# A third seven-product k pair in the gate and up projections, and three low parts formed by an accumulating DMA

## The chip, the core and the metric

The kernel runs on one core of a Trainium2 chip. The metric is the device time of one execution in microseconds (us). The core's engines are TensorE (PE in the profile, PEld for its weight loads), VectorE (DVE), ScalarE (ACT), GpSimd (POOL) and SyncE (SP); 16 DMA engines move data. SP issues the loads of the weights. GpSimd issues some small DMAs in software.

## What is computed

A trunk of two decoder layers over 256 positions of width 2048, all in float32:

```python
for layer in range(2):
    h = h + mixer(rms_norm(h, norm_mix[layer]))   # 0: sliding window + mLSTM, 1: forgetting attention
    xn = rms_norm(h, norm_ffn[layer])
    h = h + (silu(xn @ w_gate[layer]) * (xn @ w_up[layer])) @ w_down[layer]
return rms_norm(h, norm_final)
```

`w_gate` and `w_up` are 2048 x 5632, `w_down` is 5632 x 2048. The change concerns the products with `w_gate` and `w_up` alone.

## The kernel before, in words

**Two parts for one float32.** Every large product is made from operands split into a high part, the number rounded to TensorE's float32r format (`hi`), and a low part, what the rounding left (`lo = raw - hi`). A product is three matmuls: x-high with w-high, x-high with w-low, x-low with w-high (`gemm`, L164 to L166; `three`, L345 to L347).

**Chunks.** A weight chunk is two k tiles of 128 rows by 512 columns, 512 KB. `load_raw` (L85) loads it from SP's queue into one of four `raw` buffers (pool `wr`). `split_chunk` (L138) forms `hi` on ScalarE (L141) and `lo` on VectorE (L142), in pools of four buffers each (`wp`). So a load waits until a `raw` buffer has been read for the last time, a split until a `hi` and a `lo` buffer have been used for the last time by TensorE, and a matmul until its parts are there. SP issues its loads in order: one that waits holds back those behind it.

**The gate and up stage.** `ffn` (L416) cuts the 5632 columns into 11 groups of 512, in two parts of 6 and 5 groups, each part followed by its share of the product with `w_down`. `gate_up` (L352) makes one group: gate and up for both row tiles t (128 positions each), over 16 k tiles taken as eight pairs. `ORDER` (L34) says in which order, and of which kind each pair is:

- A *plain* pair (flag 0) loads one chunk of gate and one of up, splits both and runs 2 matrices x 2 k tiles x 2 row tiles x 3 = 24 matmuls.
- A *mixed* pair (flag 1) makes the same eight block products (two k tiles, two matrices, two row tiles) with seven, by a scheme of sums and differences. It loads `rg` and `ru` (L374, L375), splits `rg` as a plain chunk (L376), forms four combined weight blocks `t4` on VectorE (L378 to L381), splits one half of `ru` (L384) and `t4` in two pieces (`ht`, `lt`, L389; `split_plain` is L239 to L241), and runs 7 x 3 = 21 matmuls (L396 to L402). The matching combinations of x (`sh`, `sl`) are made once a layer by `sums_of` (L199), called from `split_scaled` in the output projection. Four of the seven products gather over the mixed pairs in four PSUM banks of their own (`mixed`, called `prod`), and are combined at the end of the group (L405 to L413).

Before, pairs 2 and 3 are mixed, in places three and six of the order; two plain pairs stand between them, two after the second and two ahead of the first. Then follow the activation (L428), the gating (L430), eight transposes (`pf`, L438) and the split of the result (L441). PSUM banks alternate: the plain banks of one group are the mixed banks of the next (`par`).

**Who orders the instructions.** The program is built with a planner that places the instructions of each engine by its own timing model; engines run their queues strictly in order, so the built order, buffer assignment included, is what runs. In this document a chunk is called by pair and matrix: 5u is the up chunk of pair 5, and 6u* one whose low part is made by DMA.

Of the kernel before, what the change touches and what calls it, by code (L numbers as in the profile page):

```python
# [7 lines left out]
F32 = mybir.dt.float32  # L8
F32R = mybir.dt.float32r
AF = mybir.ActivationFunctionType  # L10
ALU = mybir.AluOpType
# [10 lines left out]
NB = 512  # L22
# [8 lines left out]
OFF_QM, OFF_KM, OFF_VM, OFF_OM = 1536, 2048, 2560, 3584  # L31
CAP = 15.0
FILL = 24
ORDER = ((0, 0), (0, 1), (1, 2), (0, 4), (0, 5), (1, 3), (0, 6), (0, 7))  # L34
MIXED = [p for w, p in ORDER if w]
HALVES = (0, 6, 11)

# [2 lines left out]
def trunk(  # L40
# [20 lines left out]
    nc = tc.nc  # L61
# [23 lines left out]
    def load_raw(w, k0, c0, n):  # L85
        raw = wr.tile([P, CK, NB], F32, tag="raw", name="raw")
        nc.sync.dma_start(
            raw[:, :, 0:n], w[k0 * P : (k0 + CK) * P, c0 : c0 + n].rearrange("(k p) n -> p k n", p=P)
        )
        return raw  # L90
# [40 lines left out]
    gain_columns(0)  # L131


    def load_chunk(w, k0, c0, n):
        raw = ahead.pop(0) if ahead else load_raw(w, k0, c0, n)
        return split_chunk(raw, n)

    def split_chunk(raw, n):  # L138
        hi = wp.tile([P, CK, NB], F32R, tag="hi", name="hi")
        lo = wp.tile([P, CK, NB], F32R, tag="lo", name="lo")  # L140
        nc.scalar.copy(hi[:, :, 0:n], raw[:, :, 0:n])  # L141
        nc.vector.tensor_tensor(  # L142
            out=lo[:, :, 0:n], in0=raw[:, :, 0:n], in1=hi[:, :, 0:n].bitcast(F32), op=ALU.subtract
        )
        return hi, lo
# [23 lines left out]
    def x_of(k):  # L169
        return xh[:, k, :], xl[:, k, :]  # L170
# [68 lines left out]
    def split_plain(dst_h, dst_l, src):  # L239
        nc.scalar.copy(dst_h, src)  # L240
        nc.vector.tensor_tensor(out=dst_l, in0=src, in1=dst_h.bitcast(F32), op=ALU.subtract)  # L241
# [102 lines left out]
    def three(o, ah, al, hi, lo, start, stop):  # L344
        nc.tensor.matmul(o, ah, hi, start=start, stop=False)  # L345
        nc.tensor.matmul(o, ah, lo, start=False, stop=False)  # L346
        nc.tensor.matmul(o, al, hi, start=False, stop=stop)  # L347

    def bank(par, name):
        return pm.tile([P, NB], F32, tag="pm", name=name) if par else pa.tile([P, NB], F32, tag="acc", name=name)  # L350

    def gate_up(fp, sh, sl, layer, g, par):  # L352
        c0 = g * NB
        plain = [[bank(par, "acc") for _ in range(NT)] for _ in range(2)]
        mixed = None
        count = [s_[0] for s_ in ORDER]
        for pos, (w, pair) in enumerate(ORDER):
            k0 = 2 * pair
            if not w:
                for m, wt in enumerate((w_gate[layer], w_up[layer])):  # L360
                    hi, lo = load_chunk(wt, k0, c0, NB)
                    for i in range(CK):
                        ah, al = x_of(k0 + i)
                        for t in range(NT):
                            ts = slice(t * P, (t + 1) * P)
                            three(
                                plain[m][t], ah[:, ts], al[:, ts], hi[:, i, :], lo[:, i, :],
                                pos == 0 and i == 0, pos == len(ORDER) - 1 and i == CK - 1,
                            )
                continue  # L370
            first, last = 1 not in count[:pos], 1 not in count[pos + 1 :]
            if first:
                mixed = [bank(1 - par, "prod") for _ in range(4)]
            rg = load_raw(w_gate[layer], k0, c0, NB)  # L374
            ru = load_raw(w_up[layer], k0, c0, NB)  # L375
            hg, lg = split_chunk(rg, NB)  # L376
            t4 = fp.tile([P, 4, NB], F32, tag="t4", name="t4", bufs=1)
            nc.vector.tensor_tensor(out=t4[:, 0, :], in0=ru[:, 0, :], in1=rg[:, 0, :], op=ALU.subtract)  # L378
            nc.vector.tensor_tensor(out=t4[:, 1, :], in0=ru[:, 1, :], in1=ru[:, 0, :], op=ALU.subtract)  # L379
            nc.vector.tensor_tensor(out=t4[:, 2, :], in0=ru[:, 1, :], in1=t4[:, 0, :], op=ALU.subtract)  # L380
            nc.vector.tensor_tensor(out=t4[:, 3, :], in0=rg[:, 1, :], in1=t4[:, 2, :], op=ALU.subtract)  # L381
            hu = wp.tile([P, CK, NB], F32R, tag="hi", name="hi")
            lu = wp.tile([P, CK, NB], F32R, tag="lo", name="lo")
            split_plain(hu[:, 1, :], lu[:, 1, :], ru[:, 1, :])  # L384
            ht, lt = [], []
            for i in range(2):
                hs = fp.tile([P, 2, NB], F32R, tag="ht", name="ht")
                ls = fp.tile([P, 2, NB], F32R, tag="lt", name="lt")
                split_plain(hs, ls, t4[:, 2 * i : 2 * i + 2, :])  # L389
                ht += [hs[:, 0, :], hs[:, 1, :]]  # L390
                lt += [ls[:, 0, :], ls[:, 1, :]]
            j = MIXED.index(pair)
            xa, la = x_of(k0)
            xb, lb = x_of(k0 + 1)
            t0, t1 = slice(0, P), slice(P, 2 * P)
            three(mixed[0], xa[:, t0], la[:, t0], hg[:, 0, :], lg[:, 0, :], first, last)  # L396
            three(plain[0][0], xb[:, t0], lb[:, t0], hg[:, 1, :], lg[:, 1, :], False, False)
            three(plain[1][0], sh[:, j, 3, :], sl[:, j, 3, :], hu[:, 1, :], lu[:, 1, :], False, False)
            three(mixed[1], sh[:, j, 0, :], sl[:, j, 0, :], ht[0], lt[0], first, last)
            three(mixed[2], sh[:, j, 2, :], sl[:, j, 2, :], ht[1], lt[1], first, last)  # L400
            three(mixed[3], sh[:, j, 1, :], sl[:, j, 1, :], ht[2], lt[2], first, last)
            three(plain[0][1], xb[:, t1], lb[:, t1], ht[3], lt[3], False, False)  # L402
        c = fp.tile([P, 4, NB], F32, tag="c", name="c", bufs=1)
        u2 = fp.tile([P, NB], F32, tag="tmp", name="u2")
        nc.scalar.copy(c[:, 0, :], mixed[0])  # L405
        nc.vector.tensor_tensor(out=u2, in0=mixed[3], in1=c[:, 0, :], op=ALU.add)
        nc.vector.tensor_tensor(out=c[:, 1, :], in0=mixed[2], in1=u2, op=ALU.add)
        nc.vector.tensor_tensor(out=c[:, 2, :], in0=mixed[1], in1=u2, op=ALU.add)
        nc.vector.tensor_tensor(out=c[:, 3, :], in0=mixed[1], in1=c[:, 1, :], op=ALU.add)
        for m in range(2):  # L410
            for t in range(NT):
                o = c[:, 2 * m + t, :]
                nc.vector.tensor_tensor(out=o, in0=plain[m][t], in1=o, op=ALU.add)  # L413
        return c

    def ffn(layer, fp, sh, sl, eh, el, key, idx_next=None, key_next=None, finish=None):  # L416
# [4 lines left out]
        for part in range(2):  # L421
            g0, g1 = HALVES[part : part + 2]
            nk = 4 * (g1 - g0)
            for g in range(g0, g1):
                par = (g - g0 + part) % 2
                c = gate_up(fp, sh, sl, layer, g, par)
                for t in range(NT):
                    nc.scalar.activation(c[:, t, :], c[:, t, :], AF.Silu, scale=r[:, t : t + 1])  # L428
                for t in range(NT):
                    nc.vector.scalar_tensor_tensor(  # L430
                        out=c[:, t, :], in0=c[:, 2 + t, :], scalar=r[:, t : t + 1], in1=c[:, t, :], op0=ALU.mult, op1=ALU.mult
                    )
                for half in range(2):
                    pt = bank(par, "pf").rearrange("p (i q) -> p i q", i=2)
                    for i in range(2):
                        cs = (2 * half + i) * P
                        for t in range(NT):
                            nc.tensor.transpose(pt[:, i, t * P : (t + 1) * P], c[:, t, cs : cs + P], ident)  # L438
                    k = 4 * (g - g0) + 2 * half
                    if k < KT:  # L440
                        split_plain(mh[:, k : k + 2, :], ml[:, k : k + 2, :], pt)  # L441
                    else:
                        split_plain(eh[:, k - KT : k - KT + 2, :], el[:, k - KT : k - KT + 2, :], pt)
# [444 lines left out]
```

## Time and profile before

| | us |
|---|---|
| runs of the kernel (median of 3) | 2187.59 (2187.58 to 2188.13) |
| the profiled execution, its own time | 2186.29 |
| its span, first to last instruction | 2184.6 |
| TensorE busy | 2164.8 (99%) |
| VectorE busy | 1442.0 (66%) |
| ScalarE busy | 1078.5 (49%) |
| GpSimd busy | 38.4 (2%) |
| mean busy share of the DMA engines over 40 slices | 0.4 to 0.8, mostly 0.5 to 0.7 |

The granted clock of TensorE was 0.998. "Busy" for TensorE counts a matmul from its start to its modelled end; matmuls overlap, so a full row is no sign of how fast they follow each other. Groups of instructions carry the source line, the operation, the tile written and read, the shape, the count, and the busy time and mean duration of one. A wait names the engine and line that was waited for. For a DMA the profile gives the median time from issue to landing.

### The profile page before, as it was taken

The page shows a single profiled execution, that of the slowest core. Times are in us where ns is not written, and L with a number is a line of the kernel's source. Part 1 is how long each engine was busy: PE and PEld are TensorE (multiplying, and loading weights), DVE is VectorE, ACT ScalarE, POOL GpSimd, SP SyncE. Part 2 cuts the span into 40 slices and gives each one's busy share as a digit, 9 for nine tenths or more (in the row PEclk, how much of TensorE's full clock was granted, in tenths as well). Part 3 has the DMA queues.
Part 4 walks back from the last instruction along what each step waited for, and adds up shares of the span by engine and source line. Part 5 has one row for each costly group of instructions (what it writes and reads, how often), then busy time and mean ns, then how long its engine had stood idle before and what let it go on. Part 6 is the DMA issues. An engine that isn't in the chain of part 4 may idle for free.

```text
span 2184.6 us, 26574 instructions
## 1 busy us (share of the span) xinstructions
PE 2164.8 (99%) x10052; PEld 1796.9 (82%) x10052; DVE 1442.0 (66%) x1732; ACT 1078.5 (49%) x1397; POOL 38.4 (2%) x61
## 2 busy tenths in 40 slices
PE   8999999999999999999999999999999999999998
PEld 6878888888888888888888888888888888888886
DVE  5565566788754677865555555668778645777754
ACT  5565455555543455544545544555455434554543
POOL 2110000000000000000010000000000000000000
PEclk9999999999999999999999999999999999999999
DMA  8544556666666666566675565566666665666664
GB/s 258 150 147 148 171 167 184 203 186 208 187 194 193 201 192 195 190 196 190 176 229 167 164 178 157 177 184 195 208 184 197 198 193 183 208 192 199 194 191 144
DMA packets 213536, 408.33 MB, mean 187 GB/s; under 512 B 12736, under 2 KB 21024, under 8 KB 213152
## 3 DMA queue, kind: packets, MB, share of 16 engines
q1 hardware_dynamic: 212736, 402.90, 60.0%
q0 software_dynamic: 624, 3.72, 0.5%
q8 instruction: 78, 1.28, 0.2%
q14 instruction: 50, 0.41, 0.1%
q10 hardware_dynamic: 48, 0.02, 0.0%
HBM read 404.48 MB, written 2.11 MB: 186 GB/s over the span
## 4 chain that ended last, share of the span: by engine, by line
PE 98%; ACT 1%; DMA 1%; issue 0%; DVE 0%; SPq 0%; POOLq 0%; POOL 0%; ACTq 0%
PE acc L164 17%; PE acc L165 17%; PE acc L166 17%; PE acc L346 12%; PE acc L347 12%; PE acc L345 12%; PE prod L346 2%; PE prod L345 2%; PE prod L347 2%; PE pf L438 1%; DMA h<-in_x_dram 1%; PE p L269 1%; PE ptm L252 1%; PE pt L219 1%; PE po L320 1%; PE pp L312 0%
## 5 line engine op out<-in xcount | busy, mean ns | idle before, releaser
L142 DVE TENSOR_TENSOR lo<-raw,hi 128x1024 fp32r<-128x1024 f32 (+3 forms) x732 | 876.7, 1206 | 597.0 <-ACT hi L141 595.7
L141 ACT CAST hi<-raw 128x1024 fp32r<-128x1024 f32 (+3 forms) x732 | 752.3, 1034 | 825.3 <-PE acc L166 515.1
L347 PE MATMUL acc<-hi,xl 128*128 128x512 f32 x1100 | 429.7, 391 | 0.0
L346 PE MATMUL acc<-lo,xh 128*128 128x512 f32 x1100 | 428.5, 390 | 0.0
L345 PE MATMUL acc<-hi,xh 128*128 128x512 f32 x1100 | 423.8, 391 | 0.0
L164 PE MATMUL acc<-hi,mh 128*128 128x512 f32 x768 | 300.6, 392 | 1.2 <-ACT mh L240 1.2
L165 PE MATMUL acc<-lo,mh 128*128 128x512 f32 x768 | 300.7, 392 | 0.0
L166 PE MATMUL acc<-hi,ml 128*128 128x512 f32 x768 | 298.3, 390 | 0.0
L165 PE MATMUL acc<-lo,xh 128*128 128x512 f32 (+3 forms) x736 | 276.3, 376 | 0.4 <-DVE lo L142 0.4
L164 PE MATMUL acc<-hi,xh 128*128 128x512 f32 (+3 forms) x736 | 275.2, 378 | 1.2 <-ACT hi L141 1.2
L166 PE MATMUL acc<-hi,xl 128*128 128x512 f32 (+3 forms) x736 | 276.2, 376 | 0.0
L347 PEld LDWEIGHTS acc<-hi,xl 128*128 128x128 f32 x1100 | 206.5, 188 | 42.5
L346 PEld LDWEIGHTS acc<-lo,xh 128*128 128x128 f32 x1100 | 206.6, 188 | 42.4
L345 PEld LDWEIGHTS acc<-hi,xh 128*128 128x128 f32 x1100 | 206.6, 188 | 41.9
L164 PEld LDWEIGHTS acc<-hi,mh 128*128 128x128 f32 x768 | 144.2, 188 | 31.0 <-ACT mh L240 1.4
L166 PEld LDWEIGHTS acc<-hi,ml 128*128 128x128 f32 x768 | 144.2, 188 | 29.7
L165 PEld LDWEIGHTS acc<-lo,mh 128*128 128x128 f32 x768 | 144.2, 188 | 29.4
L240 ACT CAST ht<-t 128x1024 fp32r<-128x1024 f32 x88 | 92.6, 1052 | 138.9 <-DVE t L379 113.6
L164 PEld LDWEIGHTS acc<-hi,xh 128*128 128x128 f32 x736 | 138.4, 189 | 26.5 <-issue 2.0
L165 PEld LDWEIGHTS acc<-lo,xh 128*128 128x128 f32 x736 | 139.1, 189 | 24.6 <-DVE lo L142 1.1
L166 PEld LDWEIGHTS acc<-hi,xl 128*128 128x128 f32 x736 | 139.1, 189 | 24.1 <-issue 0.3
L241 DVE TENSOR_TENSOR lt<-t,ht 128x1024 fp32r<-128x1024 f32 x88 | 107.2, 1218 | 0.0
(273 smaller groups left out, 1897.5 us busy)
## 6 DMA issues: line engine op xcount, KB each, us to landing
raw<-in_w_gate_dram SPq DMA_DIRECT2D x176, 512.0 KB, 4.0
raw<-in_w_up_dram SPq DMA_DIRECT2D x176, 512.0 KB, 4.5
raw<-in_w_down_dram SPq DMA_DIRECT2D x176, 512.0 KB, 3.7
raw<-in_w_in_odd_dram SPq DMA_DIRECT2D x88, 512.0 KB, 3.8
raw<-in_w_in_even_dram SPq DMA_DIRECT2D x64, 512.0 KB, 3.9
raw<-in_w_out_even_dram SPq DMA_DIRECT2D x32, 512.0 KB, 3.7
raw<-in_w_out_odd_dram SPq DMA_DIRECT2D x32, 512.0 KB, 3.7
raw<-in_w_in_odd_dram SPq DMA_DIRECT2D x8, 272.0 KB, 2.8
```

The source lines that it names most:

```text
L141: nc.scalar.copy(hi[:, :, 0:n], raw[:, :, 0:n])
L142: nc.vector.tensor_tensor(out=lo[:, :, 0:n], in0=raw[:, :, 0:n], in1=hi[:, :, 0:n].bitcast(F32), op=ALU.subtract)
L164: nc.tensor.matmul(o, ah[:, ts], hi, start=(k == 0), stop=False)
L165: nc.tensor.matmul(o, ah[:, ts], lo, start=False, stop=False)
L166: nc.tensor.matmul(o, al[:, ts], hi, start=False, stop=(k == k_all - 1))
L219: nc.tensor.transpose(pt[:, i, t, :], h[:, t, k * P : (k + 1) * P], ident)
L240: nc.scalar.copy(dst_h, src)
L241: nc.vector.tensor_tensor(out=dst_l, in0=src, in1=dst_h.bitcast(F32), op=ALU.subtract)
L252: nc.tensor.transpose(pt[:, i, :], s_, ident)
L345: nc.tensor.matmul(o, ah, hi, start=start, stop=False)
L346: nc.tensor.matmul(o, ah, lo, start=False, stop=False)
L347: nc.tensor.matmul(o, al, hi, start=False, stop=stop)
```

## The change

Pair 1 becomes mixed as well, so three pairs of eight are, and the order now alternates: plain 0 and 4, mixed 1, plain 5, mixed 2, plain 6, mixed 3, plain 7. Of the ten plain chunks of a group, the up chunks of pairs 0, 5 and 6 get their low part in another way: ScalarE writes `-hi` into `lo`, and a DMA issued by GpSimd adds `raw` to it in place, SBUF to SBUF, 512 KB. The `raw` buffer is then held until that DMA has landed.

```diff
-ORDER = ((0, 0), (0, 1), (1, 2), (0, 4), (0, 5), (1, 3), (0, 6), (0, 7))
+ORDER = ((0, 0), (0, 4), (1, 1), (0, 5), (1, 2), (0, 6), (1, 3), (0, 7))
+BY_DMA = (0, 5, 6)
...
-    def split_chunk(raw, n):
+    def split_chunk(raw, n, by_dma=False):
         hi = wp.tile([P, CK, NB], F32R, tag="hi", name="hi")
         lo = wp.tile([P, CK, NB], F32R, tag="lo", name="lo")
         nc.scalar.copy(hi[:, :, 0:n], raw[:, :, 0:n])
+        if by_dma:
+            nc.scalar.mul(lo, hi.bitcast(F32), -1.0)
+            nc.gpsimd.dma_start(lo.bitcast(F32), raw, accum_op=ALU.add)
+            return hi, lo
...
-                    hi, lo = load_chunk(wt, k0, c0, NB)
+                    hi, lo = load_chunk(wt, k0, c0, NB, by_dma=m == 1 and pair in BY_DMA)
```

In the built programs, over 22 groups: TensorE has 9815 instructions in place of 9881 (66 matmuls of 128 x 512 fewer); VectorE 1810 in place of 1734; ScalarE 1404 in place of 1288; GpSimd 66 more, all of them the new DMAs; SP issues the same 786.

More of the change, by code (lines that the diff above doesn't have):

```diff
@@ L131, in trunk, with load_chunk @@
     gain_columns(0)
-    def load_chunk(w, k0, c0, n):
+    def load_chunk(w, k0, c0, n, by_dma=False):
         raw = ahead.pop(0) if ahead else load_raw(w, k0, c0, n)
-        return split_chunk(raw, n)
-    def split_chunk(raw, n):
+        return split_chunk(raw, n, by_dma)
+    def split_chunk(raw, n, by_dma=False):
         hi = wp.tile([P, CK, NB], F32R, tag="hi", name="hi")
```

## The prediction

> **What bounds the kernel now.** I read the shares and the chain first, then the groups, then one steady group of the gate and up stage (engines by stretch), then SP's waits and the DMA table.
>
> ```profile
> PE 2164.8 (99%) x10052; PEld 1796.9 (82%) x10052; DVE 1442.0 (66%) x1732; ACT 1078.5 (49%) x1397; POOL 38.4 (2%) x61
> PE 98%; ACT 1%; DMA 1%; issue 0%; DVE 0%; SPq 0%; POOLq 0%; POOL 0%; ACTq 0%
> ```
>
> TensorE carries 98% of the chain that ended last. A matmul fewer is time gained as long as the rest keeps up.
>
> ```profile
> core 0: us, PE busy (x) PEld busy (x) DVE busy (x) ACT busy (x) POOL busy (x), PEclk, DMA share, GB/s
> 448.45:491.57 43.12, 43.12 (x195) 35.69 (x195) 34.79 (x41) 22.25 (x26) 0.00 (x0) 1.00 0.64 195
> ```
>
> One group takes 43.1 us: TensorE full, VectorE 34.8 (81%), ScalarE 22.3, DMA engines 0.64. Less about 0.9 for the eight transposes, 186 matmuls in 42.2 us are 0.227 us each from start to start (the 0.39 of the groups overlaps).
>
> ```profile
> SPq L87 <- DVE lo L142: 1634.4, 678, 7.2
> ```
>
> This line of SP's own waits (us in total, times, longest) says what times the loads: 678 times SP waited until VectorE had read a `raw` buffer for the last time. A load starts late because its buffer comes free late, not because the memory is slow.
>
> ```profile
> DVE t L378 <- DMA raw<-in_w_up_dram: 27.2, 32, 2.0
> ```
>
> Among all waits, this shows where it tells: before 32 of 44 mixed pairs VectorE stood and waited for the up chunk. TensorE didn't notice, but the lead is short.
>
> ```profile
> raw<-in_w_up_dram SPq DMA_DIRECT2D x176, 512.0 KB, 4.5
> ...
> cb<-scratch POOLq DMA_DIRECT2D x1, 2048.0 KB, 10.4
> ...
> gain<-in_mlstm_head_gain_dram POOLq DMA_DIRECT2D x1, 512.0 KB, 7.8
> ...
> scratch<-negct POOLq DMA_DIRECT2D x1, 16.0 KB, 3.9
> ```
>
> In the DMA table the reader sees a chunk's load (4.5 us to landing) and the DMAs of GpSimd that bear on this: two large, one small.
>
> **The change, part by part.**
>
> *Matmuls.* Three fewer a group: 3 x 0.227 = 0.68 us, 22 groups: **15.0 us** gained, and TensorE's own need falls to 183 x 0.227 + 0.9 = 42.4 us a group.
>
> *VectorE.* By start-to-start times (a `lo` of 1024 every 1.13 us, a 512-wide operation every 0.60) a group loses four `lo` (-4.5: three to the DMA, and two chunks less of plain pair 1 but one more `rg`) and gains four `t4` (2.4), one half `lo` (0.6), two `lt` (2.3): 34.8 + 0.8 = 35.6 of 42.4, 84%. *ScalarE:* one `hi` fewer, three `-hi`, two `ht`, one half `hi`: 22.3 + 4.5 = 27, 63%. Neither is a bound by its sum. Without the DMA, VectorE would hold 39 of 42.4 us. GpSimd's issues took 0.55 us each (its timeline), three a group: nothing.
>
> *Sums of x.* `sums_of` runs once more a layer, in the output projection: three ScalarE operations (some 1.5 us), five VectorE ones (some 1.9). There VectorE was busy 25.4 of 40 us (stretch 310 to 350). Between 0 and 7 us in all; I take 0.
>
> *Combination.* After the last mixed pair one plain pair is left (5.4 us of TensorE, before 10.9), and the next group's plain banks are these. The copy and four additions take 0.6 + 4 x 0.6 = 3.0 us: still covered, and by the transposes too. 0.
>
> *The accumulating DMA* decides. Call X its time from issue to landing. It lies between `-hi` and the first matmul that reads `lo`, and it keeps its `raw` buffer, of which there are four. I followed in the built order which load waits for which buffer, and found a closed lap through one group, on which TensorE has no part:
>
> 1. 6u* of the last group lands; its buffer takes the load of 0g, and 0u is issued behind it: 0.6 + 4.5 = 5.1
> 2. `hi`, `-hi` on ScalarE: 2 x 1.03 = 2.1
> 3. accumulate 0u: X
> 4. its buffer takes the up chunk of pair 1: 4.5
> 5. VectorE until its last read of that pair's gate chunk: four `t4`, a `lo`, an `lt`, a half `lo`: 2.4 + 1.1 + 1.1 + 0.6, tail 0.1 = 5.3
> 6. this frees the buffers for pair 2, gate then up: 5.1
> 7. four `t4` and the `lo` of its gate chunk: 3.6
> 8. the buffer freed takes 6u: 4.5
> 9. `hi`, `-hi`: 2.1
> 10. accumulate 6u: X
>
> With ten hand-overs of some 0.07 that is 33.0 + 2X us. The group lasts the longer of this and 42.4. So up to X = 4.7 all is hidden, at X = 5.05 the gain is gone, and each further us costs 2 us a group. In the old order no buffer waited for a second transfer, and two plain pairs stood between the mixed ones; that cover is gone. Two things queue behind a late accumulate: on TensorE, which waits at the matmul that reads `lo`, all later matmuls; on SP, which waits for the buffer, all later loads. On GpSimd only `rstd`'s `r` (L196) stands among the new DMAs, needed some 30 us later.
>
> *X itself* is not in the trace. By definition an accumulate reads both tiles and writes one. Lower end: 3.7, what the quickest 512 KB load takes. Upper end: the 7.8 of `gain`, issued among the first loads, and 1.6 for a second read: 9.4. Nearest are the two rows from the middle of the kernel: 16 KB in 3.9 and 2048 KB in 10.4 give 1.64 us for each 512 KB, so 5.5 with one read, 7.2 with two. The SP loads (256 KB 2.8, 512 KB 3.8) give 2.0 for each 512 KB; with that slope `cb` leaves 2.4 fixed: 4.4 and 6.4. I take **6.6**, in the middle of the cases with two reads.
>
> The Trainium skill ("DMA: Bandwidth & Descriptors", section "Anatomy of one DMA — SWDGE (gpsimd) path") fits a DMA of this path as 2.0 us plus bytes over 436 GB/s: as an estimate 3.2 us here. "Collectives: The Full Stack" (section "The bandwidth ceiling: the fold count and why AG ≠ RS ≠ AR") says that an add costs two source reads: 4.4. By either the lap is under 42.4 and the kernel gains 15 us; this is the first rival. The trace doesn't bear the fit out: it would give 2.0, 3.2 and 6.8 for the rows of 3.9, 7.8 and 10.4.
>
> *Sum.* 33.0 + 13.2 = 46.2, 3.1 more than 43.1. The first group of each of four parts enters with its loads landed, so I count 21 laps, not 22: +65. The profiled execution took 2186.3 (span 2184.6 and 1.7 around it), the median of the runs shown is 1.3 above. 2186.3 + 65 = 2251 for its like, with the 1.3 **2253 us**.
>
> **Rivals.**
>
> *The accumulate is short (faster), 0.20.* Place: steps 3 and 10; it decides below X = 4.7. For it: source and target both lie in SBUF, and no row has such a transfer; a load with a fixed part of 1.8 us shows that a DMA can start quickly. Against: no GpSimd row is under 3.9. Time: 2187.6 - 15.0 = 2172.6, some 2 either way by the rounding of the pitch: 2170 to 2175.
>
> *Nearly even, 0.05.* X within 0.2 of 5.05: 2183 to 2192.
>
> *Loads and accumulates slow each other, 0.15.* The engines are 0.64 busy; three accumulates with twice a load's reads add some 0.2 to 0.25. 5u's accumulate runs beside loads of pairs 2 and 6. If each of the lap's four loads loses 1 us at X = 6.6, the group lasts 50.2: 21 x 7.1 = +149, 2336.
>
> *The accumulate is as slow as at the start, 0.10.* X = 9.4: 51.8, +8.7 a group, 2370.
>
> *The change doesn't do what it says.* The 66 matmuls are gone from the built order and the granted clock is 0.998, so their 0.227 us each can't come back in the others; no chance of its own.
>
> **How the numbers follow.** The forecast (X from 5.3 to 8.0: 2195 to 2311) has 0.50, the others as above. For eight in ten the range takes in the short accumulate and the crowded engines: 2170 to 2336, which leaves out the slowest case. A difference under 0.2% (4.4 us) is about what a measurement of this kernel can't tell from none: faster 0.20, same 0.05, slower 0.75.
>
> **What would show it.** Right: the new DMA's row reads 6 to 7 us; the matmul group that reads `lo` with weights from x (L351 in the new numbering) has idle time before it, released by the DMA into `lo`; TensorE is 95 to 97% busy; groups last about 46 us; VectorE's waits for the up chunk (L383) grow several times; SP waits for GpSimd's DMAs. Wrong in X alone: groups of 33.0 + 2X with another X. Wrong in the lap: groups that don't follow that sum for the X the trace shows. The short rival: X under 4.7, no idle ahead of L351, 42.4 a group. The crowded one: loads at 5.5 in place of 4.5.

## The result, and the profile after

| | us |
|---|---|
| before (median of 4 runs) | 2187.7 (2187.58 to 2188.13) |
| after (median of 4 runs) | 2209.97 (2205.38 to 2211.38) |
| ratio, 95% interval | 1.0104 [1.0092, 1.0116] |
| profiled execution of after, its span | 2205.38, 2203.7 |

The change makes the kernel 22 us slower; 65 were forecast. The granted clock was 0.997 (0.998 before). The page of after, in the order of the lines shown of before: shares, chain, the two groups of L351 that read `lo` (busy, mean ns | idle before them and who ended it), the DMA issues.

```profile
PE 2166.6 (98%) x9986; PEld 1780.0 (81%) x9986; DVE 1452.0 (66%) x1808; ACT 1183.3 (54%) x1513; POOL 95.4 (4%) x127
...
PE 72%; DMA 15%; DVE 8%; issue 2%; ACT 2%; SPq 0%; DVEq 0%; POOLq 0%; ACTq 0%; POOL 0%
...
L351 PE MATMUL acc<-lo,xh 128*128 128x512 f32 x946 | 373.7, 395 | 10.9 <-DMA lo<-raw 10.8
...
L351 PEld LDWEIGHTS acc<-lo,xh 128*128 128x128 f32 x946 | 177.5, 188 | 58.1 <-DMA lo<-raw 20.7
...
raw<-in_w_up_dram SPq DMA_DIRECT2D x176, 512.0 KB, 4.4
lo<-raw POOLq DMA_DIRECT2D x66, 512.0 KB, 5.2
```

Before, the same two groups stood at L346, and no DMA released them:

```profile
L346 PE MATMUL acc<-lo,xh 128*128 128x512 f32 x1100 | 428.5, 390 | 0.0
...
L346 PEld LDWEIGHTS acc<-lo,xh 128*128 128x128 f32 x1100 | 206.6, 188 | 42.4
```

TensorE's busy time should have fallen by 15 us with 66 matmuls less, and rose by 1.8: matmuls that start further apart overlap less, so much of the waiting is counted as busy. Its idle time, span less busy, grew from 19.8 to 37.1. The chain is the better reading: TensorE held 98% of it before and 72% now; transfers and VectorE hold 23%. The accumulate lands after 5.2 us (median; 4.5 to 6.7). Where TensorE waits for one, the chain runs through the accumulate and back to TensorE (start, us, what):

```profile
485.96 5.05 DMA lo<-raw
491.05 0.50 PE acc L351
```

In SP's own waits (us in total, times, longest) a new name stands beside VectorE's `lo`:

```profile
SPq L88 <- DVE lo L147: 1294.5, 535, 7.5
SPq L88 <- DMA lo<-raw: 178.8, 42, 8.4
```

and among all waits, VectorE's for the up chunk of a mixed pair grew from 27 to 156 us, now before all 66 of them:

```profile
DVE t L383 <- DMA raw<-in_w_up_dram: 156.2, 66, 4.7
```

By stretch, three groups of after:

```profile
core 0: us, PE busy (x) PEld busy (x) DVE busy (x) ACT busy (x) POOL busy (x), PEclk, DMA share, GB/s
490.00:622.00 132.00, 129.41 (x574) 104.53 (x573) 106.22 (x130) 79.17 (x88) 6.79 (x8) 1.00 0.75 227
```

VectorE holds 106 of 132 us (80%) and ScalarE 60%, so neither is full, and TensorE isn't either. What sets the time is a lap. A piece of it stands in the chain of waits between 542 and 562 us (start, us, what; some pieces left out):

```profile
543.49 0.61 DVE t L386
...
544.12 4.36 DMA raw<-in_w_up_dram
...
548.60 0.69 DVE t L383
...
551.22 1.13 DVE lo L147
...
553.45 5.74 DMA raw<-in_w_up_dram
...
559.31 0.69 DVE t L383
```

The last read of one mixed pair starts the next pair's load, whose landing starts the next `t4`, almost without a gap and without TensorE. The pieces up to 548.60, from pair 1 to pair 2, lie on the lap of the prediction. The load at 553.45 is 3u: it goes out behind 6u and a gate load and is no step of that lap. Followed through all 18 groups that have a predecessor in their part, the lap of the prediction reads in the trace as follows (means, us):

```
6u* landed -> 0g issued -> 0u issued         0.20 + 0.49
0u load                                      6.03
hi, -hi, until the accumulate is issued      2.54
accumulate of 0u                             5.54
-> load of 1u                                0.06 + 4.31
-> four t4 and the rest of pair 1            0.09 + 5.37
-> load of 2u                                0.03 + 4.51
t4 of pair 2, -> 6u issued behind a lo       2.86 + 1.04
load of 6u                                   3.83
hi, -hi, until the accumulate is issued      2.59
accumulate of 6u                             4.78
sum                                         44.27 = 33.95 + 10.32
```

The hand-overs (0.06, 0.09, 0.03, and 0.20 at the start) leave hardly any time in which the lap waits for something outside it. Against the 43.12 of a group before, (44.27 - 43.12) x 18 = +20.7; the profiled executions differ by 2205.38 - 2186.29 = 19.1.

### The profile page after: what moved, and what is told of

The parts are those of the page before. It is cut to its first block, busy times and chain, and to the rows that moved or that the text cites. A ratio compares the mean times of both kernels' runs of the same rounds, so it can differ in the third digit from the quotient of the medians.

```text
span 2203.7 us, 26970 instructions
## 1 busy us (share of the span) xinstructions
PE 2166.6 (98%) x9986; PEld 1780.0 (81%) x9986; DVE 1452.0 (66%) x1808; ACT 1183.3 (54%) x1513; POOL 95.4 (4%) x127
## 4 chain that ended last, share of the span: by engine, by line
PE 72%; DMA 15%; DVE 8%; issue 2%; ACT 2%; SPq 0%; DVEq 0%; POOLq 0%; ACTq 0%; POOL 0%
PE acc L169 17%; PE acc L170 16%; PE acc L171 16%; DMA raw<-in_w_up_dram 8%; PE acc L351 5%; PE acc L352 5%; DMA lo<-raw 5%; PE acc L350 5%; DVE lo L147 2%; DMA raw<-in_w_gate_dram 2%; PE prod L351 1%; PE prod L352 1%; DVE t L386 1%; DVE t L383 1%; DVE lt L246 1%
## 5 line engine op out<-in xcount | busy, mean ns | idle before, releaser
L142 ACT CAST hi<-raw 128x1024 fp32r<-128x1024 f32 (+3 forms) x710 | 730.7, 1031 | 727.3 <-PE acc L171 508.8
L147 DVE TENSOR_TENSOR lo<-raw,hi 128x1024 fp32r<-128x1024 f32 (+1 forms) x644 | 771.5, 1200 | 487.9 <-ACT hi L142 485.8
L351 PE MATMUL acc<-lo,xh 128*128 128x512 f32 x946 | 373.7, 395 | 10.9 <-DMA lo<-raw 10.8
L352 PE MATMUL acc<-hi,xl 128*128 128x512 f32 x946 | 368.8, 390 | 0.0
L350 PE MATMUL acc<-hi,xh 128*128 128x512 f32 x946 | 359.4, 391 | 0.0
L245 ACT CAST ht<-t 128x1024 fp32r<-128x1024 f32 x132 | 139.1, 1054 | 163.5 <-DVE t L384 128.4
L351 PEld LDWEIGHTS acc<-lo,xh 128*128 128x128 f32 x946 | 177.5, 188 | 58.1 <-DMA lo<-raw 20.7
L350 PEld LDWEIGHTS acc<-hi,xh 128*128 128x128 f32 x946 | 177.6, 188 | 37.0
L352 PEld LDWEIGHTS acc<-hi,xl 128*128 128x128 f32 x946 | 177.7, 188 | 35.7
L169 PEld LDWEIGHTS acc<-hi,xh 128*128 128x128 f32 x736 | 138.6, 189 | 26.4 <-issue 2.0
L170 PEld LDWEIGHTS acc<-lo,xh 128*128 128x128 f32 x736 | 139.2, 189 | 24.7 <-DVE lo L147 1.1
L171 PEld LDWEIGHTS acc<-hi,xl 128*128 128x128 f32 x736 | 139.0, 189 | 24.0 <-issue 0.3
L246 DVE TENSOR_TENSOR lt<-t,ht 128x1024 fp32r<-128x1024 f32 x132 | 157.2, 1217 | 0.0
```

The source lines that it names most:

```text
L147: nc.vector.tensor_tensor(out=lo[:, :, 0:n], in0=raw[:, :, 0:n], in1=hi[:, :, 0:n].bitcast(F32), op=ALU.subtract)
L169: nc.tensor.matmul(o, ah[:, ts], hi, start=(k == 0), stop=False)
L170: nc.tensor.matmul(o, ah[:, ts], lo, start=False, stop=False)
L171: nc.tensor.matmul(o, al[:, ts], hi, start=False, stop=(k == k_all - 1))
```

## The experiments

Each group of experiments has runs of before beside it: 2186.16 us for e1 to e4, 2186.2 for e5 to e8, 2186.45 for e9 to e11. All diffs are against after. In the expectations A is the lap theory; the rivals are named with each.

| | us, median (range) | ratio to before, 95% |
|---|---|---|
| e1: no DMA | 2192.67 (2189.79 to 2194.39) | 1.0027 [1.0016, 1.0038] |
| e2: control for e3 | 2206.43 (2199.49 to 2212.2) | 1.0091 [1.0067, 1.0115] |
| e3: five raw buffers | 2175.02 (2172.56 to 2175.64) | 0.9946 [0.9932, 0.9961] |
| e4: old order, DMA | 2193.07 (2187.94 to 2195.23) | 1.0025 [1.0016, 1.0035] |
| e5: plain copy | 2174.37 (2173.64 to 2177.38) | 0.9948 [0.9933, 0.9963] |
| e6: five buffers, no DMA | 2178.12 (2174.77 to 2180.97) | 0.9961 [0.9948, 0.9973] |
| e7: only 5u by DMA | 2174.35 (2171.2 to 2176.62) | 0.9944 [0.9929, 0.9959] |
| e8: smaller pieces | 2216.53 (2215.79 to 2217.62) | 1.0139 [1.0123, 1.0154] |
| e9: 0u and 6u | 2173.7 (2173.2 to 2177.79) | 0.9945 [0.993, 0.9959] |
| e10: only 0u | 2204.76 (2202.62 to 2212.18) | 1.0088 [1.0069, 1.0108] |
| e11: only 6u | 2171.01 (2169.89 to 2174.37) | 0.9926 [0.991, 0.9943] |

**e2 and e3: a fifth raw buffer.** The room for it comes from scratch tiles: two names of them get one buffer in place of two, and one tile is placed in another buffer. e2 does that alone. The first diff shows two places of e2, the second what e3 adds.

```diff
-            junk = sm.tile([P, NB], F32, tag="junk", name="junk")
+            junk = sm.tile([P, NB], F32, tag="junk", name="junk", bufs=1)
...
-        full = pool.tile([P, 2, NT, P], F32, tag="tmp", name="full")
+        big = pool.tile([P, 4, NB], F32, tag="c", name="full", bufs=1)
+        full = big[:, 0, :].rearrange("p (i t q) -> p i t q", i=2, t=NT)
```
```diff
-    wr = ctx.enter_context(tc.tile_pool(name="wr", bufs=4))
+    wr = ctx.enter_context(tc.tile_pool(name="wr", bufs=5))
```

> Control for the next kernel: the changed kernel with two small scratch tiles single in place of double and one placed in another buffer, raw buffers still four. All theories: as the changed kernel, 2205 to 2213.

> The same with five raw buffers in place of four; the accumulating DMAs stay. Theory A: the lap is broken (the chunk that a late accumulate holds back is no longer the next one needed), groups fall to 42.4 to 42.8, 2172 to 2182. Theory B: no change, 2205 to 2213. Theory C: no change or little, 2200 to 2213, since the same bytes cross the same DMA engines; loads stay at 4.5 and more.

e2 stayed with after, e3 gained 31 us over it. From the page of e3, and the same stretch as of after:

```profile
lo<-raw POOLq DMA_DIRECT2D x66, 512.0 KB, 5.8
```
```profile
490.00:622.00 132.00, 132.00 (x598) 109.28 (x597) 107.47 (x129) 81.28 (x91) 6.80 (x8) 1.00 0.79 235
```

The accumulates take longer than in after (5.8), the DMA engines are busier (0.79), the up chunks take 4.8 in place of 4.4, and yet TensorE is full there, and most groups last 42.4 us, the need that was worked out. So neither the length of the accumulate nor the crowding costs anything by itself; four buffers make them cost. Loads and accumulates that slow each other are thus not the loss by themselves; what they may add to a lap is seen in e5. The theory that a third mixed pair is too much for VectorE and ScalarE (B) falls as well, since e3 keeps that pair.

**e1 and e6: no DMA, with four and with five buffers.**

```diff
-BY_DMA = (0, 5, 6)
+BY_DMA = ()
```

> Third mixed pair and new order kept, all low parts on VectorE again (no accumulating DMA). Theory A (the lap through the raw buffers: 33.0 + 2X a group, X = 5.2 measured): without X the lap is about 33, below TensorE's 42.4; VectorE needs 39.0 of 42.4. Expects 2172 to 2182, faster than before (2187.7). Theory B (the third mixed pair itself is too much for VectorE and ScalarE in this order, the DMA has nothing to do with it): 2210 or more, since VectorE has more to do here. Theory C (the DMA engines are crowded and all loads are late): like A, faster than before, with the share of the DMA engines back at 0.63 and loads at 4.0 to 4.5.

> Five raw buffers and no accumulating DMA: all low parts on VectorE. What made the kernel without the DMA take 2193 and not 2172? Theory V (VectorE, 39.0 of 42.4 us a group, is late in its own order): a fifth buffer changes little, 2186 to 2195. Theory R (its raw buffers come free late, here too): 2172 to 2180, like the changed kernel with five buffers.

e1 missed: 2172 to 2182 was expected, and it came out slower than before. With all the `lo` on VectorE, the buffers are held by VectorE's queue in place of the DMA. SP's own waits in e1:

```profile
SPq L88 <- DVE lo L147: 1369.3, 605, 8.1
SPq L88 <- DVE t L385: 186.0, 34, 8.4
```

The second line isn't among the first ten names of after. The chain of e1 gives VectorE 17% and transfers 13%. A fifth buffer (e6) lets the buffers come free in time again, as theory R had it, and takes back 14.5 of the 17.6 us that separate e1 from e3; the other 3, with VectorE at 89% (117.12 of 132 us), are not clear of the noise, as the intervals of e3 and e6 overlap. So a third mixed pair needs relief of some kind: VectorE's time or a buffer.

**e4: the old order with the DMA.**

```diff
-ORDER = ((0, 0), (0, 4), (1, 1), (0, 5), (1, 2), (0, 6), (1, 3), (0, 7))
+ORDER = ((0, 0), (0, 1), (1, 2), (0, 4), (0, 5), (1, 3), (0, 6), (0, 7))
```

> The accumulating DMA alone: the old order with two mixed pairs (66 matmuls more than the changed kernel), up chunks of pairs 0, 5 and 6 by DMA. Theory A: what counts is how many accumulates follow each other through the buffers in a group; TensorE's need is 43.1 and two plain pairs stand between the mixed ones, so 2185 to 2200, at most some 10 over before. Theory C: the share of the DMA engines rises to 0.75 as in the changed kernel and loads are as late: 2200 to 2225.

2193.07, as the lap theory had it. The accumulates (5.4 us) alone hardly disturb the old order: most of its groups last about 43.1 us, TensorE's need there, at a DMA share of 0.78 to 0.79. Of the 7 us over before, 3 lie in the first group of each layer (45.1 and 44.2 us from first matmul to first matmul), most of the rest in a few other groups. Held against what TensorE needs (before, less 15.0 us where the 66 matmuls are gone), e4 (old order, accumulates) loses 7 us, e1 (new order, none) about 22, and after, with both, 37.

**e5: a copy in place of the accumulate.** `lo` then holds `raw`. The order on every engine is that of after, instruction by instruction.

```diff
-            nc.gpsimd.dma_start(lo.bitcast(F32), raw, accum_op=ALU.add)
+            nc.gpsimd.dma_start(lo.bitcast(F32), raw)
```

> The changed kernel with a plain copy of raw into lo in place of the accumulate (this leaves out the addition: the low part is raw, not raw - hi). Every engine's order is that of the changed kernel, only the DMA differs. Theory A (lap of 33 + 2X): the time follows X, 21 laps x 2 = 42 us for each us of X. If the second read is what X consists of beyond a plain transfer, X falls from 5.2 to 4.0 to 4.6 and the time from 2210 to 2173 to 2185; if X stays 5.2, 2205 to 2213. Theory C (crowded DMA engines): the time goes with the share of the DMA engines, whatever X is: with a share of 0.70 some 2195 to 2205.

The cleanest of the tests, since no engine's order and no buffer changes, only the DMA. The page of e5, chain and DMA:

```profile
PE 98%; ACT 1%; DMA 1%; issue 0%; DVE 0%; SPq 0%; POOLq 0%; POOL 0%; ACTq 0%
...
lo<-raw POOLq DMA_DIRECT2D x66, 512.0 KB, 3.6
```

X fell from 5.2 to 3.6 (medians) and the whole loss was gone: TensorE has 98% of the chain, and a group lasts 42.40 to 42.43 us but for the first of a part. The lap's terms sum to 42.4 there, with 1.2 us of waiting at the first hand-over, where after has 0.2: 0g now mostly goes out behind 7u, whose buffer VectorE frees, so the lap no longer sets the pace. Two things shortened it. Its two accumulates went from 10.32 to 8.25 us (4.66 at 0u, 3.59 at 6u), and its loads of 1u, 2u and 6u lost 1.0 together. The first alone brings 44.27 to 42.2, just under TensorE's 42.4, so X is enough; the quicker loads, at a DMA share of 0.66 in place of 0.75, suggest that crowding had a small part in the lap. An accumulate is thus 1.6 us longer than a copy here by the medians (0.9 at 0u, 1.2 at 6u, 2.2 at 5u by the means).

**e8: the same bytes in smaller pieces**, to lengthen X. One element in 256 is left without the sum.

```diff
-            nc.gpsimd.dma_start(lo.bitcast(F32), raw, accum_op=ALU.add)
+            pieces = [z.rearrange("p k (a n) -> p (k a) n", a=2)[:, :, 0 : NB // 2 - 1] for z in (lo.bitcast(F32), raw)]
+            nc.gpsimd.dma_start(*pieces, accum_op=ALU.add)
```

> The accumulate in four rows of 255 elements a partition in place of one of 1024 (this leaves out one element in 256 of the sum, whose low part is then -hi). More and smaller packets, so X should rise. Theory A: 42 us for each us of X over 5.2, so with X = 6.2 about 2250; with X = 5.2 2205 to 2220, since the order differs slightly. Theory C: the bytes are the same, so 2205 to 2220 whatever X is.

X rose to 5.8 (median), the time by 6.6 us. On the lap the two accumulates went from 10.32 to 11.48, the sum from 44.27 to 44.73: the direction of the lap theory, less than its size, as the other terms shrank by 0.7. Of that, 0.6 are quicker loads of 1u, 2u and 6u. The order was planned anew here and differs a little, though the lap closes through the same buffers, so this dose doesn't measure the slope.

**e7, e9, e10, e11: which of the three accumulates.**

```diff
-BY_DMA = (0, 5, 6)
+BY_DMA = (5,)
```

So in e7; `(0, 6)` in e9, `(0,)` in e10, `(6,)` in e11.

> Four raw buffers, third mixed pair, and only the up chunk of pair 5 by DMA, which is the one of the three that is no step of the lap. Theory A: no X stands in the lap; between the kernel with no DMA (2193) and the bound by TensorE (2172): 2175 to 2193. Theory D (each accumulate costs its own share wherever it stands, a third of what the three cost over no DMA): 2193 + 6 = 2199 or more.

> BY_DMA = (0, 6), four raw buffers: 5u's low part on VectorE, both accumulates of the lap kept. Lap theory (A): the two accumulates that lie on the lap are both there, so the group keeps about 33.95 + 2 x 5.1 = 44.2 us, up to 1 more because 5u's lo (1.13 us) now stands in VectorE's queue between pair 1 and pair 2: 2205 to 2225, no better than with three accumulates. Count theory (D): each accumulate costs alike, two of three: (2210 - 2174) x 2/3 + 2174 = 2198, or less. If the fifth accumulate was itself the cost, 2174.

> BY_DMA = (0,): one accumulate on the lap; 6u's place on it is taken by VectorE's lo behind hi (1.1 + 1.1 us in place of 2.6 + 4.8). Lap theory (A): 44.3 - 7.4 + 2.2 = 39.1 by its own terms, under TensorE's 42.4: 2172 to 2180, unless VectorE's queue (with five lo of up chunks, as in the kernel without accumulates) holds a raw buffer longer: up to 2193. Count theory (D): one of three, 2186.

> BY_DMA = (6,): the other accumulate of the lap alone; 0u's place is taken by hi and VectorE's lo (2.2 us in place of 2.5 + 5.5). Lap theory (A): 44.3 - 8.0 + 2.2 = 38.5, under TensorE's 42.4: 2172 to 2180, with the same reserve up to 2193. Count theory (D): 2186.

e7 and e11 came within 1 us of the ranges of the lap theory, just under them. e9 and e10 didn't, and they also refute the theory of a price for each accumulate: two of them cost nothing, one of the two by itself costs 31 us. What I had held constant in these two expectations is the order. Read from the built programs, load by load, it isn't:

- In after, 5u's buffer is held by its accumulate, and the planner gives 6u the buffer of pair 2's gate chunk. That closes the lap. In e9, 5u's buffer is read out by VectorE and 6u gets that one: step 8 of the prediction no longer follows step 7, the lap isn't there, and groups last 42.42 us with X at 5.3.
- In e10 another lap closes: 0u, 1u, 2u and 3u take the same buffer in turn, and the next 0g gets that of 3g, which is last read once 3u is there. Its chain of waits (start, us, what), one lap from accumulate to accumulate:

```profile
528.59 5.78 DMA lo<-raw
...
534.42 5.01 DMA raw<-in_w_up_dram
...
541.48 1.13 DVE lo L147
...
546.72 4.23 DMA raw<-in_w_up_dram
...
552.36 1.14 DVE lo L147
...
556.47 4.37 DMA raw<-in_w_up_dram
...
564.59 1.15 DVE lo L147
...
565.75 5.29 DMA raw<-in_w_gate_dram
...
574.89 6.33 DMA lo<-raw
```

From 528.59 to 574.89 are 46.3 us, and TensorE is on none of it. From one accumulate to the next the 18 laps of e10 take 44.0 us on average, so this is one of the longer ones. Here it is VectorE's stay between two loads that lengthens the lap: with 5u and 6u back on VectorE, a `lo` of a plain chunk (1.13 to 1.15) stands between the `t4` each time, and 1u is held 7.3 us after landing (4.9 in after and e9). Replace this lap's `-hi` and accumulate (1.1 + 0.3 + 5.8) by a `lo` on VectorE (1.1) and it is 40, under TensorE's 42.4. e11 does that, and its groups last 42.4; but in its order 0u takes the buffer of 6u*, so it is no pure test of this sum.

e11 is the fastest kernel of the study: 15.4 us under before, which is the 15.0 that 66 matmuls were worth. It differs from after by one tuple.

## Why the prediction was right in direction and wrong in size

**Right: what bounds, and the kind of loss.** TensorE's need of 42.4 us was met wherever the feed kept up (42.40 to 42.46 in most groups of e3, e5 and e9), and the gain of 15.0 appears whole in e11. VectorE and ScalarE are no bounds by their sums: 107.47 and 81.28 of the 132 us of e3 are 34.5 and 26.1 a group of 42.43 (35.6 and 27 predicted). The lap runs through the steps named, in their order, with a constant part of 33.95 for 33.0. e5 and e3 show it from two sides: shorten X, or add a buffer, and the loss is gone. The signs named in advance came: idle time ahead of L351 released by the DMA, L383's waits, SP's waits for the DMA. TensorE's busy share didn't fall to 95 to 97%: 98%, for the reason given above.

**Wrong: the size of X, in the step headed "X itself".** 6.6 was taken; the lap's two accumulates took 5.54 and 4.78, 10.3 in place of 13.2. That is 2.9 us a group too much. The slope was about right: 1.64 us for one more pass over 512 KB, and 5.2 less 3.6 is 1.6, with some luck, as the means of the three chunks lie between 0.9 and 2.2. The fixed part was not: 6.6 holds 3.3 beside two passes, 5.2 only 1.9. As the base of a transfer from SBUF to SBUF I took GpSimd's rows from the middle of the kernel, whose 16 KB one writes to DRAM (3.9 us). The copy of e5 does 512 KB in 3.6; less one pass of 1.64 leaves about 2.0. The load with a fixed part of 1.8, which the text held for the short rival, was the nearer row.

**Wrong as well, the other way: the constant part and the number of laps.** With the X that was measured, the prediction's lap would be 33.0 + 10.3 = 43.3, a loss of 4 us in place of 22. The constant part was 33.95, mainly because the load of 0u took 6.03 us in place of 4.5, and this 0.95 is most of the loss that was left. The laps were miscounted: four first groups that enter with their loads landed leave 18 of 22, not 21. In order: 21 x 3.1 = +65 becomes +4 with the right X, +24 with the right constant part, +21 with 18 laps. So that a clear loss was foreseen is in part luck: without the error in X, the error in the constant part would have hidden most of it. The lower end of the forecast is also 3 us off by its own sum: X = 5.3 gives 2198, not 2195.

The fit in the Trainium skill ("DMA: Bandwidth & Descriptors", section "Anatomy of one DMA — SWDGE (gpsimd) path"), 3.2 us for one pass, is close to the 3.6 of e5, and two source reads by "Collectives: The Full Stack" (section "The bandwidth ceiling: the fold count and why AG ≠ RS ≠ AR"), an estimate of 4.4, are 0.8 under the 5.2 of after. The measured values decide; that an accumulate takes longer than a copy, as a second read would make it, they bear out. I set the fit aside because other rows disagreed with it, rows of other kinds of transfer. The gain by which it was a rival didn't come: X measures above the 4.7 up to which all was hidden, by 0.1 at 6u and 0.8 at 0u.

**The rivals.** The short accumulate failed by half a microsecond a transfer; e5, with a copy, shows the time that it named (2174.37). Nearly even had its condition met, X within 0.2 of 5.05 (5.16 is the mean of the lap's two), and yet the time was not 2183 to 2192, because the constant part was longer. An X of 9.4 didn't occur: the longest of 66 was 6.7. Crowding as the cause fell with e3: the DMA share did rise, to 0.75 to 0.77, but the gate loads only from 4.0 to 4.5, and the up loads not at all (4.5, 4.4). Of the lap's loads only 0u's is long (6.03), issued right behind 0g's.

**Wrong without effect on the time: "Without the DMA, VectorE would hold 39 of 42.4 us".** The sum held (e6: 89%), but I took it as harmless in the expectation of e1. In e1 VectorE's queue held buffers long enough to cost time, though its sum was under TensorE's.

**Incomplete: the lap as a property of three accumulates.** I read it from one built order and carried it to others. e9 and e10 show that which buffer a load gets, and so which lap closes, changes with every edit that the planner sees. For after itself the lap stands, on e5, whose order is the same. For e10 it rests on its chain; a copy in e10's order wasn't tried. e7 and e11 have orders of their own too, so their times are weak evidence for the lap of after. Why the loads of e8 are quicker stays open, and with it the slope above X of 5.2.

## What to carry to other kernels

Where a few buffers feed a full engine, write down which load takes whose buffer, follow it until it closes, and compare the sum of the lap (transfers included) with the engine's need: busy shares show nothing of it, and one lap longer by 1 us is paid in every iteration. A slow step then belongs on a buffer that no closed lap uses, or the ring gets one buffer more, and each such edit means reading the new order again. Base the fixed cost of a transfer on a row with the same kind of source and target.

## What the runs showed of the hardware

- An accumulate from SBUF into SBUF by GpSimd's queue takes 5.2 us for 512 KB (4.5 to 6.7), a copy 3.6 (2.8 to 6.2), and its packets take twice the DMA engines' time. The queue's row in after and in e5 (packets, MB, share of 16 engines):

```profile
q0 software_dynamic: 10128, 38.33, 8.8%
```
```profile
q0 software_dynamic: 10128, 38.33, 4.4%
```

- GpSimd is busy 0.85 us to issue one accumulate and about 0.54 to issue a copy (4.30 us for 8 in e5's three groups).
- Four pieces of 1020 bytes in place of one row of 4 KB a partition cost the accumulate 0.6 us (5.8 for 5.2), with 35472 packets on that queue in place of 10128.
